# A streaming encoder step on one core: order of the last feed-forward part, PSUM copies for the GELU inputs, and projections woven between recurrent branches

## The chip, the core and the metric

The kernel runs on one core of a Trainium2 chip. A core has five engines that run side by side and meet through semaphores: TensorE (PE, matrix products into PSUM; PEld are its weight loads), VectorE (DVE), ScalarE (ACT), GpSimd (POOL) and SyncE (SP), which here issues all DMA transfers. Each engine executes its own list of instructions strictly in the order written; an instruction that waits holds up everything behind it on that engine. The metric is the device time of one execution in microseconds (us), taken as the median of several.

## The reference

One step of a two-layer encoder with 1024 columns of a prompt and 64 columns of a sample that continues a cache. Layer 0 mixes with two kinds of attention (A and B); layer 1 mixes with forgetting attention (C) and a gated recurrent branch (D). A gated feed-forward network (FFN) follows each mixer, and a norm ends it.

```python
def rmsnorm(x, g):
    return x * lax.rsqrt(jnp.mean(x * x, axis=-1, keepdims=True) + EPS) * g
def swiglu(h, w1, w3, w2):
    return (jax.nn.silu(h @ w1) * (h @ w3)) @ w2
# layer 1, mixer C and D
    cq, ck, cv, cf, dx, dg = split_cols(h @ w_in, CD_SIZES)
    logf = log_sigmoid(cf + c_f_bias); F = jnp.cumsum(logf, axis=1)
    # C: s = q k^T * SCALE + F_q - F_k, causal softmax, times v (8 heads)
    # D: width-4 causal convolution u of dx, then for every channel
    r = sigmoid(u @ w_a + b_a); i = sigmoid(u @ w_x + b_x)      # blocks of 64
    log_a = -RG_C * r * softplus(-lam); a = exp(log_a)
    b = sqrt(-expm1(2.0 * log_a)) * (i * u)                     # h_t = a_t h_(t-1) + b_t
    o_d = hseq * gelu(dg)
    out = concatenate([o_c, o_d]) @ w_out
# each layer: x += mixer(rmsnorm(x)); x += swiglu(rmsnorm(x)); at the end rmsnorm(x)
```

All values are fp32. The model width is 1024, the recurrent width 512, the FFN's hidden width 2816.

## The kernel before, in words

The 1088 columns (1024 of the prompt and 64 of the sample) lie along the free dimension and are cut into three chunks of 384, 384 and 320 columns (`CH`). Features lie on the partitions, in blocks of 128. Every large product is made of three matrix multiplications on rounded halves (high times high, high times low, low times high), so an output block of one chunk with 8 input blocks costs 24 matmuls; this text calls that a chunk product. `split` makes such halves: ACT copies the high half (L217) and another engine subtracts it (L218). `loadw` loads a weight block with one DMA into a ring of two raw buffers, and then splits it: ACT L217, POOL L218.

The order of the program: `layer_ab` (attention A and B and its output product), `ffn(0)`, `layer_cd` (the four recurrent branches, then four C units of two heads each, then the output product), `ffn(1)`, the final norm. The program is written as Python code; a scheduler turns it into one list per engine, and these lists are fixed before the run. Matmul results go to a ring of eight PSUM banks in the FFN (`mmf`) and in the recurrent branches (`mmd`), and to a ring of two banks (`mma`) in the projections of attention units.

*Last FFN part.* `ffn` adds the second product in three parts of hidden blocks. Parts 0 and 1 go block by block, all three chunks with each weight block. The last part, of 6 blocks (L1126 to L1128, 18 matmuls for a block and chunk), goes chunk by chunk: for each chunk all eight output blocks, each with its own load of the weight block (`second`, 128x768), 24 loads in all. DVE adds the result to x (L1156); ACT squares it, and DVE or POOL adds up the squares (`addsq`, L274 and L275). After output block 3 of chunks 1 and 2 stands `rms` of the chunk before: one matmul over the partitions (L256), then Ln and Exp on ACT. After chunk 1 comes `after(0, ..)`: in layer 0 that is `between`, which loads the first weights of layer 1 (`early_weights`), stores x of the chunk and norms it (`norm`: DVE L284, split on ACT, DVE and POOL). The rest (`rms` of chunk 2, and chunks 1 and 2 of `between` or `final`) comes after.

*Recurrent branches.* For m = 0 to 3, `d_in` computes dx of branch m (a chunk product for each chunk, L234 to L236) and ACT copies it from PSUM (L1272); `d_conv` makes u from it on DVE (four passes and a split); `d_gelu` computes the gate product dg (L234 to L236) and GELU of it: Square on ACT (L1282), POOL L1283, DVE L1284, Tanh on ACT (L1287, L1289), DVE L1290. For branches 1 to 3 the operand of Square, L1284 and L1290 is the PSUM bank itself; for branch 0 ACT copies it to SBUF first. `d_close` multiplies u with the two gate matrices (L1317 to L1319, 18 matmuls), takes Sigmoid on ACT (L1320), then goes on: POOL L1328, ACT Tanh (L1330), Exp, Square, Ln, Exp (L1335 to L1339), DVE, the scan over time on DVE (L1342, L1343) and the product with the gate (L1346); its result is stored in `o_spill`. The program's order is d_in(m), d_close(m-1), d_conv(m), d_gelu(m).

*First attention unit.* `units` then runs the projections q, k and v of the first C unit (`proj`, L246, 24 matmuls for a chunk). `d_close` of branch 3 is put in where k's weights are loaded. From then on `run` weaves the items of one attention unit (scores L457 and L458, DVE L469, Exp on ACT, transposes L574, value products L499 and L500) with the projections of the next unit. Before the first scores the bias of the unit's two heads must be there: two loads of `forget_rows` (stored earlier by the forget scan) and POOL L762; that bias lies where the buffers of the last branch lay.

## Time and profile before

Three executions took 2762.43, 2769.10 and 2769.78 us (median 2769.1). The profile is of one more execution that took 2767.11 us; its span on the core, from first to last instruction, is 2765.3 us, so 1.8 us lie around it.

| | us | share of span |
|---|---|---|
| PE matmuls | 2613.0 | 94% |
| DVE | 1367.8 | 49% |
| POOL | 1253.5 | 45% |
| ACT | 1222.7 | 44% |
| chain that ended last, steps on PE | | 76% |
| mean clock granted to PE | | 0.979 |

Busy time counts the time in which an engine has an instruction in hand. The chain is followed back from the last instruction to what released it each time. The span is long and has many stages; the change touches the stretch from about 1350 to 1640 us (end of the first FFN, recurrent branches, first attention unit) and the last 60 us, and the text reads those stretches on their own. In rows of groups, the columns are line, engine, operation, output and input with their shapes, count, then busy us and mean ns of one, then idle time of the engine just before and what ended it. In rows of the timeline they are start, duration and the instruction, with the idle time before it and what ended that in brackets.

### The profile page before, as it was taken

To read this page: it belongs to the slowest core of one execution; us is meant where nothing else is said; L and a number is where in the kernel's file an instruction comes from. 1 tells how busy PE (TensorE), PEld (TensorE's weight loads), DVE (VectorE), ACT (ScalarE), POOL (GpSimd) and SP (SyncE) were. 2 spreads that over 40 slices of the span, in tenths; PEclk is the share of its full clock that TensorE was granted. 3 is DMA by queue.
4 is the path that set the end of the run, shared out by engine and by line. 5 is a ranking of instruction groups with operands and counts; after the bars stand their busy time and mean duration, and the time that the engine had idled before them with its cause. 6 is when DMAs were issued, how large, how long until landed. Compare 5 with 4: busy or idle time off the path is not lost.

```text
span 2765.3 us, 45216 instructions
## 1 busy us (share of the span) xinstructions
PE 2613.0 (94%) x17614; PEld 2536.4 (92%) x17614; DVE 1367.8 (49%) x2739; ACT 1222.7 (44%) x2395; POOL 1253.5 (45%) x990
## 2 busy tenths in 40 slices
PE   6999999988899999999988789998989999999997
PEld 5899999888899999999978779988989999999997
DVE  7666666767332332522257547777853233242225
ACT  5666677754323323311245546676432323331113
POOL 5222222323766676312474333352466667642135
PEclk9999999999999999999999899999999999999998
DMA  6222222352222221532342432234222221244224
GB/s 203 73 68 77 68 64 58 109 156 72 81 95 71 81 84 63 186 110 78 101 148 34 46 89 80 76 121 149 94 78 87 79 87 63 87 149 139 71 66 144
DMA packets 119287, 261.63 MB, mean 95 GB/s; under 512 B 21896, under 2 KB 71312, under 8 KB 119072
## 3 DMA queue, kind: packets, MB, share of 16 engines
q1 hardware_dynamic: 119072, 258.74, 30.8%
q8 instruction: 138, 2.26, 0.3%
q14 instruction: 77, 0.63, 0.1%
HBM read 190.49 MB, written 65.43 MB: 93 GB/s over the span
## 4 chain that ended last, share of the span: by engine, by line
PE 76%; DVE 8%; ACT 6%; DMA 4%; POOL 3%; issue 3%; SPq 0%; DVEq 0%; ACTq 0%; POOLq 0%
PE banks L1026 32%; PE banks L246 16%; PE banks L1127 6%; PE banks L1128 6%; PE banks L1126 6%; PE banks L574 3%; ACT split_arena L217 2%; DVE split_arena L218 2%; POOL split_arena L218 2%; PE banks L457 2%; PE banks L458 1%; PE banks L499 1%; PE banks L500 1%; DMA arena<-o_spill 1%; DVE arena L275 1%
## 5 line engine op out<-in xcount | busy, mean ns | idle before, releaser
L218 POOL TENSOR_TENSOR split_arena<-arena,split_arena 128x512 fp32r<-128x512 f32 (+5 forms) x530 | 824.5, 1559 | 1176.0 <-ACT split_arena L217 1099.4
L217 ACT ACTIVATE split_arena<-arena 128x512 fp32r<-128x512 f32 (+10 forms) x693 | 486.6, 714 | 1111.8 <-PE banks L1026 441.0
L1026 PE MATMUL banks<-split_arena 128*128 128x272 f32 x7392 | 946.3, 291 | 29.0 <-DVE split_arena L218 13.3
L1026 PEld LDWEIGHTS banks<-split_arena 128*128 128x128 f32 x7392 | 941.1, 190 | 34.2 <-DVE split_arena L218 14.8
L246 PE MATMUL banks<-split_arena 128*128 128x384 f32 (+1 forms) x3528 | 663.1, 335 | 23.3 <-DVE arena L1290 8.0
L246 PEld LDWEIGHTS banks<-split_arena 128*128 128x128 f32 x3528 | 587.3, 191 | 32.6 <-DVE arena L1290 8.3
L1126 PE MATMUL banks<-split_arena 128*128 128x384 f32 (+1 forms) x1056 | 347.3, 329 | 5.2 <-DVE arena L1093 3.6
L1128 PE MATMUL banks<-split_arena 128*128 128x384 f32 (+1 forms) x1056 | 347.1, 329 | 3.6 <-POOL split_arena L218 3.6
L1127 PE MATMUL banks<-split_arena 128*128 128x384 f32 (+1 forms) x1056 | 346.3, 328 | 1.7 <-DVE split_arena L218 1.7
L218 DVE TENSOR_TENSOR split_arena<-banks,split_arena 128x512 fp32r<-128x512 f32 (+4 forms) x312 | 167.6, 542 | 96.8 <-ACT split_arena L217 93.9
L1126 PEld LDWEIGHTS banks<-split_arena 128*128 128x128 f32 x1056 | 199.7, 189 | 7.5 <-issue 4.0
L1128 PEld LDWEIGHTS banks<-split_arena 128*128 128x128 f32 x1056 | 199.8, 189 | 5.0 <-POOL split_arena L218 4.9
L1127 PEld LDWEIGHTS banks<-split_arena 128*128 128x128 f32 x1056 | 199.8, 189 | 2.4 <-DVE split_arena L218 2.0
L218 DVE TENSOR_TENSOR split_arena<-arena,split_arena 128x1088 fp32r<-128x1088 f32 (+8 forms) x163 | 163.4, 1013 | 76.8 <-ACT split_arena L217 75.9
L469 DVE CUSTOM_DVE_ANT_0 arena<-banks,arena 128x384 f32<-128x384 f32 (+4 forms) x368 | 175.6, 494 | 45.7 <-PE banks L458 39.8
L217 ACT ACTIVATE split_arena<-banks 128x512 fp32r<-128x512 f32 (+4 forms) x312 | 146.6, 476 | 106.5 <-PE banks L574 45.3
L1034 DVE TENSOR_TENSOR arena<-banks,arena 128x544 f32<-128x544 f32 (+1 forms) x46 | 32.1, 699 | 301.2 <-PE banks L1026 301.2
L1147 DVE TENSOR_TENSOR arena<-banks,arena 128x384 f32<-128x384 f32 (+1 forms) x96 | 51.3, 535 | 251.4 <-PE banks L1128 251.2
L471 ACT ACTIVATE arena<-arena 128x640 f32<-128x640 f32 (+8 forms) x216 | 156.3, 724 | 43.3 <-DVE arena L469 41.9
L574 PE MATMUL banks<-arena 128*128 128x128 f32 (+2 forms) x828 | 134.1, 273 | 14.1 <-DVE arena L490 7.1
L574 PEld LDWEIGHTS banks<-arena 128*128 128x128 f32 (+2 forms) x828 | 95.9, 140 | 31.5 <-DVE arena L490 10.5
L457 PE MATMUL banks<-split_arena 128*128 128x256 f32 (+3 forms) x312 | 112.7, 363 | 3.0 <-issue 2.0
(167 smaller groups left out, 3059.7 us busy)
## 6 DMA issues: line engine op xcount, KB each, us to landing
arena<-in_w_dram SPq DMA_DIRECT2D x120, 512.0 KB, 3.5
h_spill<-arena SPq DMA_DIRECT2D x22, 1088.0 KB, 4.2
arena<-h_spill SPq DMA_DIRECT2D x44, 544.0 KB, 4.7
arena<-in_w_dram SPq DMA_DIRECT2D x48, 384.0 KB, 3.2
arena<-in_abw_dram SPq DMA_DIRECT2D x24, 512.0 KB, 3.7
arena<-in_cdw_dram SPq DMA_DIRECT2D x20, 512.0 KB, 3.9
x_spill<-arena SPq DMA_DIRECT2D x48, 192.0 KB, 2.2
arena<-x_spill SPq DMA_DIRECT2D x16, 544.0 KB, 4.9
```

What stands on the lines that cost most here:

```text
L217: self.nc.scalar.activation(hi, x, AF.Copy)
L218: return sub.tensor_tensor(lo, x, hi.bitcast(F32), op=ALU.subtract)
L246: self.pe = self.nc.tensor.matmul(ps, x[:, k], y[k][:, c0:c0 + n], start=a and i == 0, stop=z and i == 2).ins
L457: nc.tensor.matmul(ps[:, :mw], qd[:, q0:q0 + m], kk[:, k0 + s:k0 + s + mw], start=True, stop=False)
L469: nc.vector.tensor_tensor_reduce(o, p, t, -1.0, low, ALU.add, ALU.min, to)
L471: nc.scalar.activation(sb, sb, AF.Exp, bias=st[:, 0:1], scale=-1.0, accum_out=st[:, 1:2])
L574: nc.tensor.transpose(pt[:r, t * nq + s * m:t * nq + s * m + m], src, self.ident[:m, :m])
L1026: nc.tensor.matmul(bank[:, p], l[:, k], r[:, k, x], start=first and i == 0, stop=k == 3 and i == 2, skip_group_check=True)
L1126: nc.tensor.matmul(ps, wh, h[:, c0:c0 + n], start=j == j0, stop=False)
L1127: nc.tensor.matmul(ps, wh, lo[:, c0:c0 + n], start=False, stop=False)
L1128: nc.tensor.matmul(ps, wl, h[:, c0:c0 + n], start=False, stop=j == j1 - 1)
L1147: nc.vector.tensor_tensor(xs, ps, xs, op=ALU.add)
```

## The change

Three things are done.

1. **Last FFN part.** Its loop goes over the eight output blocks with chunks 0 and 1 each, then over blocks 6 and 7 (whose weights are still there) and 0 to 5 (loaded again) with chunk 2: 14 loads of a weight block where there were 24. `rms` of chunks 0 and 1 both stand after the second block of chunk 2, followed by `after(0, ..)`, and in layer 1 also `after(1, ..)` two blocks later. Adding up squares in chunk 2 is given to DVE for the first three blocks and alternates after that. The first weights of layer 1 are loaded while blocks 3 and on are computed.
2. **GELU inputs.** `d_gate` (new) computes dg of branches 1 to 3 and ACT copies it from PSUM to SBUF (L1319 of the new program). GELU of branch m-1 is computed from that copy in the next turn, after the gate products of m-1. `d_close` is cut into `d_gates` (products and Sigmoid) and the rest. The ring of the branches' weights has three places instead of four.
3. **First attention unit.** Its six chunk products of q and k are computed inside the recurrent branches, two in each turn (q0 and q1, q2 and k0, k1 and k2), through the eight-bank ring. `d_gates(3)`, GELU of branch 3 and the rest of branch 3 stand ahead of the v projection, which is all that is left of `proj` for this unit.

No product is added or removed: the number of matmuls is the same, 17,579.

```diff
-        self.w_d = at([0, 1024, R_V[0], R_PT]), at([2048, 3072, R_V[1], R_PT + 1024])
+        self.w_d = at([0, 1024, R_PT]), at([2048, 3072, R_PT + 1024])
...
-    def proj(self, u, d, wq, wk, wv, pair, outs):
+    def proj(self, u, d, wq, wk, wv, pair, outs, only_v=False):
...
-        w = self.loadw(wq, self.w_a)
...
+        if not only_v:
+            w = self.loadw(wq, self.w_a)
...
-    def clear_ql(self):
...
             self.start(d, *units[0][2])
-            nb = units[0][1]()
         else:
-            for kind, _ in self.proj(0, d, *units[0][2]):
-                if kind == "w" and between:
-                    between(self.pe)
-                    between = None
-            nb = units[0][1]()
+            for kind, _ in self.proj(0, d, *units[0][2], True):
+                if kind == "w":
+                    between()
+                    self.clear_ql(1)
+        nb = units[0][1]()
...
-    def ffn(self, l, after):
+    def ffn(self, l, after, early=lambda: None):
...
-        more = [(ci, m) for ci in range(3) for m in range(8)]
-        lasts = []
...
                 xs = self.x[m][ci]
                 nc.vector.tensor_tensor(xs, ps, xs, op=ALU.add)
-        rs = []
-        for ci, (c0, n) in enumerate(CH):
-            for m in range(8):
-                if 8 * ci + m + 1 < len(more):
-                    lasts.append(second(2, more[8 * ci + m + 1][1], ends, nc.gpsimd))
+
+        blocks = list(range(8)) + list(range(6))
+        uses = [(i, (0, 1)) for i in range(8)] + [(i, (2,)) for i in range(6, 14)]
+        ws.append(second(2, 1, ends, nc.gpsimd))
+        for q, (i, cs) in enumerate(uses):
+            if q + 2 < 9 or q > 8:
+                m = len(ws)
+                if m < 14:
+                    ws.append(second(2, blocks[m], ends, nc.gpsimd))
+            if q == 3:
+                early()
+            m = blocks[i]
+            for ci in cs:
+                c0, n = CH[ci]
                 ps = self.mmf.get()[:, :n]
-                gemm2(ps, lasts.pop(0), 2, c0, n)
+                gemm2(ps, ws[i], 2, c0, n)
                 xs = self.x[m][ci]
                 nc.vector.tensor_tensor(xs, ps, xs, op=ALU.add)
                 if ci < 2:
                     self.addsq(ci, m, xs, (nc.vector, nc.gpsimd)[m % 2])
+                elif q < 11:
+                    self.addsq(2, m, xs, nc.vector, first=q == 8)
                 else:
-                    self.addsq(ci, m, xs, (nc.gpsimd, nc.vector)[m % 2], 2 - 2 * (m % 2), m < 2)
-                if ci > 0 and m == 3:
-                    rs.append(self.rms(ci - 1))
-            if ci == 1:
-                after(0, rs[0])
+                    self.addsq(2, m, xs, (nc.gpsimd, nc.vector)[q % 2], 2 - 2 * (q % 2), q == 11)
+            if q == 9:
+                r0 = self.rms(0)
+                r1 = self.rms(1, to=self.v(F_END, 384))
+                after(0, r0)
+            if q == 11 and l:
+                after(1, r1)
 
         def rest():
-            r = self.rms(2, [2, 0], self.acc[1])
-            after(1, rs[1])
+            r = self.rms(2, [2, 0], self.v(F_END + 384, 384))
+            if not l:
+                after(1, r1)
             after(2, r)
         return rest
 
     def between(self, ci, r):
         c0, n = CH[ci]
-        if ci == 0:
-            self.early_weights()
         for k in range(8):
             self.dma(self.xTd[k * 128:k * 128 + 128, c0:c0 + n], self.x[k][ci])
         self.norm(ci, 8, r=r)
...
-        b["uh"], b["ul"] = self.r(R_Q[m % 2], T), self.r(R_Q[m % 2] + T, T)
+        b["uh"], b["ul"] = (self.r(o, T) for o in ((R_Q[1], R_Q[1] + T), (R_Q[1] + 2 * T, R_QL[1]))[m % 2])
...
-        nc.scalar.activation(dx[:, 3 + c0:3 + c0 + npr], ps[:, :npr], AF.Copy)
+        b["in"] = nc.scalar.activation(dx[:, 3 + c0:3 + c0 + npr], ps[:, :npr], AF.Copy).ins
...
-    def d_gelu(self, b, ci, ps=None):
+    def d_gelu(self, b, ci):
         nc = self.nc
         c0, n = CH[ci]
-        if ps is None:
-            ps, _ = self.d_products(b["w"][1], ci)
+        ps = b["G"][:, c0:c0 + n]
         z2, z = self.stg.get()[:, :n], self.nat.get()[:, :n]
         nc.scalar.activation(z2, ps, AF.Square)
...
-    def d_close(self, b, m, after):
-        nc, O = self.nc, self.O
+    def d_gate(self, b):
+
+        for ci, (c0, n) in enumerate(CH):
+            ps, _ = self.d_products(b["w"][1], ci)
+            self.nc.scalar.activation(b["G"][:, c0:c0 + n], ps, AF.Copy)
+
+
+    def d_gates(self, b, m, after):
+        nc = self.nc
         R = self.D.get()
         b["slots"].insert(0, R)
-        R, u = R[:, 0:T], b["u"]
-        Ig = b["dx"][:, 0:T]
+        b["R"] = R = R[:, 0:T]
+        b["I"] = Ig = b["dx"][:, 0:T]
         for gi, (dst, bc) in enumerate(((R, 5), (Ig, 6))):
             hi, lo = self.gates[2 * m + gi]
             for c0, n in CH:
...
+    def d_close(self, b, m):
+        nc, O = self.nc, self.O
+        R, Ig, u = b["R"], b["I"], b["u"]
...
-    def recurrent(self, pending):
+    def recurrent(self, pending, d, wq, wk, ckT, outs, keep):
...
-        gates = []
         for ci in range(3):
             (p, _), f, (g, _) = step(ci) if ci else first
...
-        for ci in range(3):
-            self.d_gelu(b, ci, gates[ci])
+        stg, self.stg2 = self.stg, Ring(self.M, [F_STG2, F_STG2 + 384], 384)
+
+        def between():
+
+            w = self.loadw(wq, [Ring(self.MR, [R_K[0] + 1024 * i], 1024) for i in range(2)])
+            for ci in range(3):
+                ps, _ = self.d_products(w, ci)
+                self.put_q(d, *CH[ci], ps)
+                if ci == 1:
+                    v = self.loadw(wk, [Ring(self.MR, [R_V[i]], 1024) for i in range(2)])
+                    self.cached_k(d, ckT)
+                yield
+            for ci in range(3):
+                ps, _ = self.d_products(v, ci)
+                self.stg = self.stg2
+                self.new_k(d, *CH[ci], ps, outs, keep)
+                self.stg = stg
+                yield
+        self.clear_ql(0)
+        more = between()
         for m in range(1, 4):
             nb = self.d_open(m)
             for ci in range(3):
                 self.d_in(nb, ci)
-            self.d_close(b, m - 1, nb["pe"])
+            next(more)
+            self.d_gates(b, m - 1, nb["pe"])
+            with self.tc.issue_after(nb["in"]):
+                for ci in range(3):
+                    self.d_gelu(b, ci)
+            self.d_gate(nb)
+            self.d_close(b, m - 1)
+            next(more)
             self.d_conv(nb, m)
+            b = nb
+
+        def rest():
+            self.d_gates(b, 3, b["pe"])
             for ci in range(3):
-                self.d_gelu(nb, ci)
-            b = nb
-        return lambda after: self.d_close(b, 3, after)
+                self.d_gelu(b, ci)
+            self.d_close(b, 3)
+        return rest
 
     def layer_cd(self, pending):
         nc, I, O = self.nc, self.I, self.O
         W = I["cdw"]
         self.lastu = 3
-        rest = self.recurrent(pending)
+        rest = self.recurrent(pending, self.qkv_views(0), W[0], W[4], I["cckT"][0], (O["c_kT"][0], O["sc_kT"][0]), 0)
```

The lists of the engines are the same up to the last FFN part of layer 0. Three places show what moves after it.

On DVE at the turn from chunk 1 to chunk 2 of the last FFN part of layer 0 (sum with x: L1156 before, L1165 now; adding squares: L275, now L277; norm of chunk 0: L284 and L218, now L286 and L220), before:

```order
L284 SCALAR_TENSOR_TENSOR arena<-arena 128x384
L218 TENSOR_TENSOR split_arena<-arena,split_arena 128x384
L1156 TENSOR_TENSOR arena<-banks,arena 128x384
L284 SCALAR_TENSOR_TENSOR arena<-arena 128x384
L275 TENSOR_TENSOR arena<-arena 128x384
L284 SCALAR_TENSOR_TENSOR arena<-arena 128x384 x2
L1156 TENSOR_TENSOR arena<-banks,arena 128x384
L218 TENSOR_TENSOR split_arena<-arena,split_arena 128x384
L284 SCALAR_TENSOR_TENSOR arena<-arena 128x384 x2
L218 TENSOR_TENSOR split_arena<-arena,split_arena 128x384
L1156 TENSOR_TENSOR arena<-banks,arena 128x320
```

and now:

```order
L1165 TENSOR_TENSOR arena<-banks,arena 128x384
L277 TENSOR_TENSOR arena<-arena 128x384
L1165 TENSOR_TENSOR arena<-banks,arena 128x384 x2
L1165 TENSOR_TENSOR arena<-banks,arena 128x320 x2
L277 TENSOR_TENSOR arena<-arena 128x320
L286 SCALAR_TENSOR_TENSOR arena<-arena 128x384 x3
L220 TENSOR_TENSOR split_arena<-arena,split_arena 128x384
L1165 TENSOR_TENSOR arena<-banks,arena 128x320
L220 TENSOR_TENSOR split_arena<-arena,split_arena 128x384
```

The norm's first products and splits stood ahead of the first sum of chunk 2 (128x320); two of these sums and one of its squares now stand ahead of them.

On ACT in the turn of a recurrent branch (Sigmoid of the gates: L1320, now L1337; copies of dx from PSUM: L1272, now L1284; Square and Tanh of GELU: L1282, L1287, L1289, now L1293, L1298, L1300; the chain behind the gates: L1330 to L1339, now L1351 to L1360), before, from the end of one chain to the next gates:

```order
L1282 ACTIVATE arena<-banks 128x384
L217 ACTIVATE split_arena<-arena 128x1024
L1287 ACTIVATE arena<-arena 128x384
L1282 ACTIVATE arena<-banks 128x320
L1289 ACTIVATE arena<-arena 128x384
L1289 ACTIVATE arena<-arena 128x320
L1272 ACTIVATE arena<-banks 128x384 x2
L217 ACTIVATE split_arena<-arena 128x1024
L1272 ACTIVATE arena<-banks 128x256
L1274 ACTIVATE arena<-banks 128x64
L1320 ACTIVATE arena<-banks,arena 128x384 x2
```

and now, from the middle of a chain on:

```order
L1360 ACTIVATE arena<-arena 128x384
L1319 ACTIVATE arena<-banks 128x384
L1360 ACTIVATE arena<-arena 128x384
L1357 ACTIVATE arena<-arena 128x320
L219 ACTIVATE split_arena<-arena 128x1024
L1359 ACTIVATE arena<-arena 128x320
L219 ACTIVATE split_arena<-arena 128x64
L1360 ACTIVATE arena<-arena 128x320
L1293 ACTIVATE arena<-arena 128x384
L1319 ACTIVATE arena<-banks 128x320
L219 ACTIVATE split_arena<-arena 128x1024
L176 ACT_TABLE_LOAD
```

GELU's Square read the bank itself between the products; now a copy of the bank (L1319) stands there, among the steps of the chain, and Square reads SBUF.

On PE from the last gate products to the first scores of the first attention unit (gates: L1317 to L1319, now L1334 to L1336; projections: L246, now L248; transposes of v: L356 and L359, now L358 and L361; scores: L457 and L458, now L460 and L461), before:

```order
L1318 MATMUL banks<-split_arena 128x320
L1319 MATMUL banks<-split_arena 128x320
L246 MATMUL banks<-split_arena 128x384 x48
L246 MATMUL banks<-split_arena 128x320 x48
L246 MATMUL banks<-split_arena 128x384 x4
L356 MATMUL banks<-arena 128x128 x2
L246 MATMUL banks<-split_arena 128x384 x8
L359 MATMUL banks<-arena 64x128
L246 MATMUL banks<-split_arena 128x384 x17
L356 MATMUL banks<-arena 128x128 x3
L246 MATMUL banks<-split_arena 128x384 x19
L457 MATMUL banks<-split_arena 64x320
```

and now:

```order
L1335 MATMUL banks<-split_arena 128x320
L1336 MATMUL banks<-split_arena 128x320
L248 MATMUL banks<-split_arena 128x320 x24
L248 MATMUL banks<-split_arena 128x384 x24
L460 MATMUL banks<-split_arena 64x320
L358 MATMUL banks<-arena 128x128 x2
L248 MATMUL banks<-split_arena 128x384 x15
L358 MATMUL banks<-arena 128x128 x2
L361 MATMUL banks<-arena 64x128
L358 MATMUL banks<-arena 128x128
L248 MATMUL banks<-split_arena 128x384 x9
L461 MATMUL banks<-split_arena 64x320
```

Behind the last gate products stood the products of k and v; now v's stand there alone (24 of 320 columns and 48 of 384), and the next rows belong to the second unit's q.

42 lines of the change are left out of this document (22 added, 20 removed).

## The prediction

> **What bounds the kernel now.** I read the chain of waits first, then cut the span into stages by time, then asked who PE waited for in the stage that changes. Page, chain that ended last:
>
> ```profile
> PE 76%; DVE 8%; ACT 6%; DMA 4%; POOL 3%; issue 3%; SPq 0%; DVEq 0%; ACTq 0%; POOLq 0%
> ```
>
> PE sets the end, so a gain must be idle or slow time of PE. Stage by stage (stretch, its length, busy us of PE, PEld, DVE, ACT, POOL with counts, granted clock, DMA share, GB/s):
>
> ```profile
> 1403.80:1436.70 32.90, 22.90 (x128) 20.92 (x129) 17.98 (x23) 14.66 (x27) 24.18 (x20) 0.84 0.52 148
> 1483.00:1519.70 36.70, 28.81 (x168) 27.65 (x168) 26.36 (x30) 22.10 (x43) 13.11 (x13) 0.98 0.22 31
> 1519.70:1554.70 35.00, 29.76 (x163) 28.71 (x163) 21.29 (x22) 19.07 (x37) 14.98 (x10) 0.92 0.37 47
> 1554.70:1579.20 24.50, 15.63 (x84) 15.11 (x84) 15.92 (x22) 17.16 (x35) 5.71 (x7) 0.87 0.36 44
> 1597.50:1639.20 41.70, 32.44 (x175) 30.79 (x173) 16.59 (x23) 19.56 (x41) 17.84 (x19) 0.92 0.35 98
> 1403.80:1639.20 235.40, 190.16 (x1055) 180.15 (x1055) 139.32 (x170) 120.30 (x243) 106.42 (x104) 0.92 0.36 72
> 2727.00:2751.50 24.50, 19.54 (x126) 18.20 (x124) 11.88 (x19) 10.10 (x17) 14.37 (x9) 0.98 0.44 140
> 2751.50:2765.30 13.80, 2.50 (x4) 1.18 (x4) 5.54 (x8) 2.49 (x5) 3.85 (x4) 0.50 0.35 124
> ```
>
> From the last FFN chunk of layer 0 to the first attention scores PE is idle 235.4 - 190.2 = 45 us, and slowed while busy (clock 0.84 and 0.87). No other engine is full there. Its waits in that stretch (waiter, releaser, total, times, longest):
>
> ```profile
> PE banks L1317 <- DVE arena L1290: 8.7, 4, 3.7
> PE banks L246 <- DVE arena L1290: 8.0, 1, 8.0
> PE banks L256 <- POOL arena L275: 6.6, 1, 6.6
> PE banks L246 <- ACT split_arena L304: 6.3, 2, 4.0
> PE banks L356 <- DVE arena L350: 2.9, 1, 2.9
> ```
>
> PE waits for PSUM banks that GELU holds (L1290) and for the squares of a chunk (L256 on L275). Both are what the change works on.
>
> **Last FFN part of layer 0.** Timeline rows of PE, and groups between 1403.8 and 1436.7:
>
> ```profile
> 1399.77 0.33 PE L1128 MATMUL banks<-split_arena 128*128 128x384 f32 x1
> 1400.81 0.33 PE L1128 MATMUL banks<-split_arena 128*128 128x384 f32 x1
> 1400.99 0.31 PE L1126 MATMUL banks<-split_arena 128*128 128x320 f32 x1
> 1403.47 0.31 PE L1128 MATMUL banks<-split_arena 128*128 128x320 f32 x1
> 1410.43 1.65 PE L256 MATMUL banks<-arena 128*128 128x384 f32 x2 [6.65 <-POOL arena L275]
> 1416.29 0.47 PE L1127 MATMUL banks<-split_arena 128*128 128x320 f32 x1
> 1418.95 0.47 PE L1128 MATMUL banks<-split_arena 128*128 128x320 f32 x1
> ```
>
> ```profile
> L218 POOL TENSOR_TENSOR split_arena<-arena,split_arena 128x768 fp32r<-128x768 f32 x7 | 12.9, 1843 | 6.4 <-ACT split_arena L217 6.4
> L217 ACT ACTIVATE split_arena<-arena 128x768 fp32r<-128x768 f32 x7 | 5.9, 841 | 9.3 <-DMA arena<-in_w_dram 9.3
> L284 DVE SCALAR_TENSOR_TENSOR arena<-arena 128x384 f32<-128x384 f32 x8 | 8.7, 1123 | 0.2
> ```
>
> A matmul of 384 columns starts every 1.04/6 = 0.173 us, one of 320 every 2.48/17 = 0.146; after the 6.65 us stall 2.66/10 = 0.266. Hence a chunk product of 24 costs 4.16 or 3.51 us, three chunks 11.8, the 18 gate products 3.0. Chunk 2 has 8 x 18 matmuls, 21.0 us, and with the two `rms` 22.7. It ran from 1400.99 to 1436.7, 35.7 us. So 13.0 us is all that can be got. Now weights come 14 times, not 24: with chunks 0 and 1 a block lasts 18 x 2 x 0.173 = 6.2 us on PE against 1.84 on POOL and 0.84 on ACT for its split, and the first two blocks of chunk 2 need no load. But chunk 0's norm, eight L284 of 1.12 us with splits between them, now begins 6 blocks (15.8 us) ahead of the branches' first product: about 9 us of L284 and 4 splits and sums leave 0 to 4 us uncovered, and POOL's last squares may hold `rms` a little. I take a gain of **10** (5 to 13).
>
> **The recurrent turns.** PE rows, with idle time in brackets:
>
> ```profile
> 1483.24 0.44 PE L1317 MATMUL banks<-split_arena 128*128 128x384 f32 x1 [0.97 <-ACT split_arena L217]
> ...
> 1579.24 1.01 PE L246 MATMUL banks<-split_arena 128*128 128x384 f32 x2 [8.01 <-DVE arena L1290]
> ...
> 1597.48 0.34 PE L1317 MATMUL banks<-split_arena 128*128 128x384 f32 x1
> ```
>
> From the end of d_in(1), 0.97 us ahead of the first row, to gates(3) it takes 1597.5 - 1482.3 = 115.2 us. After the change PE has there three gates (3 x 3.0), d_in of branches 2 and 3, dg of 1 to 3, and q and k: 9 + 7 x 11.8 = 91.6 us. One turn (35.0 us above, with 26.6 us of products: two times 11.8 and 3.0) gains two chunk products, about 8 us, which is what its GELU chain left open. A bank of dg is freed by one copy and not after a whole GELU; the chain behind it no longer stands in front of PE. Left are waits for weights (L217, L218) and for u; the small ones now, about 1 us each (0.97 above), come three to five times: 2.7 (0 to 8). So gates(3) come 115.2 - 91.6 - 2.7 = **20.9** us earlier over and above the first part (15 to 24).
>
> Three copies a branch are added on ACT, which is busy 19.1 of 35.0 us in such a turn; a copy is of Square's kind (0.5 us), 1.5 us a turn. It hides behind ACT's idle 15.9 us; uncovered it would cost 4.5.
>
> **From gates(3) to the scores.** What is late next is the closing chain of branch 3, for the bias of the first scores lies in its buffers. Rows of ACT, DVE, SP (start, issue time) and POOL in order of time, and GELU's Tanh as a group:
>
> ```profile
> 1599.54 0.76 ACT arena L1320 x2
> ...
> 1613.95 2.99 DVE L1342 TENSOR_TENSOR_SCAN arena<-arena 128x1024 f32<-128x1024 f32 x1
> 1617.93 3.42 DVE L1346 SCALAR_TENSOR_TENSOR arena<-arena 128x1088 f32<-128x1088 f32 x1
> 1621.38 0.33 SPq L170 DMA_DIRECT2D o_spill<-arena  x1
> 1632.04 0.33 SPq L170 DMA_DIRECT2D arena<-forget_rows  x1
> 1636.61 0.31 POOL L762 TENSOR_TENSOR arena<-arena 64x64 f32<-64x64 f32 x1 [5.64 <-DMA arena<-forget_rows]
> 1639.23 0.47 DVE L469 CUSTOM_DVE_ANT_0 arena<-banks,arena 64x320 f32<-64x320 f32 x1
> ```
>
> ```profile
> L1289 ACT ACTIVATE arena<-arena 128x384 f32<-128x384 f32 x4 | 2.1, 524 | 7.3 <-DVE arena L1284 7.3
> ```
>
> 41.7 us pass from gates(3) to the first score. None of it is removed, and GELU of branch 3 is now inside it (six ACT passes of about 0.5 us: 3 us, with DVE's and POOL's parts beside them), and the chain of branch 2, whose gates stand only 18 us of products ahead (3.0, dg 11.8 and the last of k 3.5), runs into it. Behind the waiting score on DVE stand all later scores, and Exp on ACT waits for them. I take **4** us longer (1 to 8). PE has less under it: it was busy 32.4 of those 41.7 us; now it has the gates, v (11.8) and 30 matmuls of the second unit's q (5.2), 20 in all, and waits 25 us. Those 30 stood behind the first scores before; they fill idle time and are saved later, as far as PE bounds the unit: **3** us gained (0 to 5). PE then starts slow, as after the 6.65 us stall, where some 20 matmuls cost 0.12 us more: **2** lost (1 to 3).
>
> **End of layer 1.** The last 8 blocks of chunk 2 take 24.5 us now, limited by their loads; at 2.63 us each they take 21.0. But DVE gets 16 products of the final norm in front of the sums of chunk 2, and after the last product `rms`, `final` and its stores (13.8 us above) stay as they are. I take **1** gained (4 gained to 2 lost).
>
> **Sum.** -10 - 20.9 + 4 - 3 + 2 - 1 = -29, so 2738 against the profiled execution's own 2767.1. Its median is 2769.1, 2.0 above it; I state the forecast for the median: **2740**.
>
> **A rule against it.** Two sums of squares on DVE, of 384 and 320 columns:
>
> ```profile
> 1403.44 0.56 DVE L275 TENSOR_TENSOR arena<-arena 128x384 f32<-128x384 f32 x1
> ...
> 1426.22 2.06 DVE L275 TENSOR_TENSOR arena<-arena 128x320 f32<-128x320 f32 x1 [0.54 <-ACT arena L274]
> ```
>
> The second, smaller one ran beside POOL's L218 and took 1.5 us longer. The Trainium skill, SBUF — State Buffer, "SBUF: two separate sides", says that a DVE instruction with two SBUF inputs and a GpSimd instruction exclude each other for their whole length; a PSUM operand avoids that. These rows agree. As a mechanism here: L1284 and L1290 had one operand in PSUM, now both lie in SBUF. If each of branch 3's six is held by 1.5 us, its chain grows by 9 us, to 2749.
>
> **The rivals.** *(a) The held GELU*: the closing chain of branch 3 grows by six times 1.5 us on top of the 4: 2740 + 9 = 2749. For it: the pair of rows. Against it: POOL is busy only 15.0 of 35.0 us in a turn. *(b) PE full*: no stall in the turns, all 13 us of the FFN, and the scores wait no longer than before: -13 - 23.6 - 5 + 2 - 4 = -43.6 from 2769.1, 2726. Against it: each weight load still comes in order behind others on SP. *(c) ACT's list as the bound, slower than before.* The copies that free dg's banks stand among the steps of the closing chain on ACT. That chain takes from Sigmoid to scan some 14 us (1599.5 to 1613.9) and waits for POOL and DVE inside. If a copy must wait for it in each of three turns and the eight banks are full by then, a turn is its 35 us of products and 14 of chain: 3 x 14 = 42 lost on top of the other terms, 2740 + 42 = 2782. It decides once the chain ends more than the turn's later products (dg's two chunks, 8 us, and q or k's, 4) after the copy's bank is full. Against it: these banks and products give 12 us of slack of those 14. *(d) The change does not do what it says*: the scheduler's lists show q and k within the turns, so only the FFN's part might fail, if `rms` waits as before: 2740 + 10 = 2750.
>
> **How the numbers follow.** Chances: forecast 0.62 (own range 2728 to 2752), (a) 0.14, (b) 0.08, (c) 0.08, (d) 0.08. The range of 8 in 10 takes in (a), (d) and part of (b), and the bad ends of the turns and the FFN (6 + 5 us) with the better part of the closing chain's: 2724 to 2759. What can be told from no change here is 0.3%, 8.3 us: faster means under 2760.8. Of (c) I put 0.07 slower and 0.01 within; of the forecast, (a) and (d) 0.08 fall within, where their bad ends meet. Faster 0.84, same 0.09, slower 0.07.
>
> **What would show it.** Right: chunk 2 of the first FFN's last part within 27 us; waits of PE for L1290's successor gone; turns of 35 to 38 us with PE over 95%; gates(3) near 1567; the first score near 1612, with PE idle over 20 us ahead of it. Wrong: PE waiting for a dg copy that follows a chain step on ACT (c); L1290's successor at 2 us (a); the first score within 42 us of gates(3) (b); `rms` still waiting over 5 us (d). The forecast fails most easily at the 20.9 of the turns, should PE wait for u or a weight load.

## The result and the profile after

The changed kernel takes 2751.15 us (median of 4, 2749.40 to 2753.34) against 2769.44 us (4 runs) before. The ratio is 0.9933, 95% interval 0.9921 to 0.9945: faster by 18 us (15 to 22). The forecast was 2740 (2724 to 2759): the direction and the range hold, and 11 us of the gain are missing.

The profiled execution of the change took 2753.34 us, the slowest of its four and 2.2 above their median; that of the kernel before lay 2.3 below its own. So the two spans, 2765.3 and 2751.6, differ by 13.7 only, and 13.7 + 2.2 + 2.3 = 18.2 is the difference of the medians. The steps below add up to the 13.7 but for rounding. The page of the change, engines and chain that ended last:

```profile
span 2751.6 us, 45123 instructions
PE 2614.3 (95%) x17614; PEld 2541.5 (92%) x17614; DVE 1353.8 (49%) x2741; ACT 1209.4 (44%) x2384; POOL 1223.8 (44%) x968
PE 9%; DVE 0%; ACT 0%; DMA 0%; POOL 0%; DVEq 0%; issue 0%; ACTq 0%; SPq 0%
```

PE is as busy as before (2613.0), with 17,614 matmuls in both profiles (17,579 above is not what they count), so idle time went. The chain is of no use here: its shares add up to 9%, so it was not followed back to the stretch that changed. The stages have to be cut by time again. The change by stage (columns as in the prediction; the third row takes in the tail of the second):

```profile
1401.00:1428.30 27.30, 25.51 (x167) 24.72 (x165) 18.92 (x22) 13.97 (x25) 17.50 (x14) 1.00 0.44 128
1428.30:1481.40 53.10, 49.81 (x294) 45.91 (x293) 36.19 (x54) 26.61 (x57) 27.95 (x33) 1.00 0.25 52
1477.20:1585.20 108.00, 95.67 (x560) 94.14 (x558) 66.36 (x70) 66.44 (x133) 46.55 (x36) 0.95 0.36 51
1528.70:1565.30 36.60, 35.39 (x212) 35.07 (x211) 19.79 (x24) 21.42 (x44) 14.47 (x13) 1.00 0.47 63
1585.20:1626.60 41.40, 27.29 (x135) 25.59 (x135) 22.65 (x33) 22.79 (x52) 19.79 (x20) 0.84 0.46 90
```

The marks between the stages are first products of PE: d_in(0), gates(3), and the first score on DVE. The end of d_in(1) is that of its last product.

| stretch | before | after | difference | forecast |
|---|---|---|---|---|
| up to d_in(0) | 1436.7 | 1428.3 | -8.4 | -10 |
| d_in(0) to the end of d_in(1) | 45.6 | 48.9 | +3.3 | 0 |
| end of d_in(1) to gates(3) | 115.2 | 108.0 | -7.2 | -20.9 |
| gates(3) to the first score | 41.8 | 41.4 | -0.4 | +4 |
| first score to the end | 1126.1 | 1125.0 | -1.1 | -2 (-3 + 2 - 1) |

The first line came nearly as forecast: from the first product of chunk 2 (1403.84) it takes 24.5 us where it took 35.7, and `rms` no longer waits. These 11.2 us show as 8.4 in the table because chunk 2 begins 2.8 us later in this profile than before (1401.0). That is not shown to come from the change: in the profiles of the twelve kernels here that have the new order, chunk 2 begins between 1398.4 and 1403.8, so single profiles of one order differ there by 5 us. Of the second line 3 us are PE waits for the halves of chunk 1's norm (the two L237 lines below). The hole is in the third. PE has 91.6 us of products there and took 108.0: 12.3 idle, and 4.1 in which products ran slower than their usual pitch. The turn from 1528.7 to 1565.3 shows what was forecast: 36.6 us with PE busy for 35.4, 97%. Who PE waited for from 1401 to 1640:

```profile
PE banks L236 <- DVE split_arena L329: 9.6, 2, 8.4
PE banks L460 <- DVE arena L472: 8.0, 1, 8.0
PE banks L248 <- ACT arena L1337: 3.1, 1, 3.1
PE banks L237 <- DVE split_arena L220: 2.4, 1, 2.4
...
PE banks L237 <- POOL split_arena L220: 0.6, 1, 0.6
```

One wait of 8.4 us stands out. It is in the first of the new turns, at the second chunk of dg(1), and slows PE after it. PE's rows:

```profile
1499.04 0.69 PE L236 MATMUL banks<-split_arena 128*128 128x384 f32 x1 [8.42 <-DVE split_arena L329]
1499.53 0.52 PE L237 MATMUL banks<-split_arena 128*128 128x384 f32 x1
...
1504.01 0.45 PE L236 MATMUL banks<-split_arena 128*128 128x384 f32 x1
1504.30 0.34 PE L237 MATMUL banks<-split_arena 128*128 128x384 f32 x1
1504.47 0.33 PE L238 MATMUL banks<-split_arena 128*128 128x384 f32 x1
```

From 1499.53 to 1504.01 stand 14 products 0.32 us apart, then 0.17 again: 14 times 0.15 is 2.1 us lost on top of the 8.4.

The bank that PE needs holds the first product of q, which came first in this turn; L329 of `put_q` is the instruction that has read it last. What stood ahead of L329 on DVE:

```profile
1484.55 5.16 DVE L1244 TENSOR_TENSOR_SCAN arena<-arena 8x1024 f32<-8x1024 f32 x2 [0.24 <-DMA out_c_logfT_dram<-arena]
1489.74 0.99 DVE L1245 TENSOR_SCALAR arena<-arena 8x1344 f32<-8x1344 f32 x1
...
1492.79 0.55 DVE L1295 TENSOR_TENSOR arena<-arena 128x384 f32<-128x384 f32 x1
1496.00 0.56 DVE L1295 TENSOR_TENSOR arena<-arena 128x384 f32<-128x384 f32 x1 [2.66 <-POOL arena L1294]
1496.48 1.35 DVE L1311 SCALAR_TENSOR_TENSOR arena<-arena 128x1091 f32<-128x1091 f32 x1
1497.86 1.12 DVE L329 SCALAR_TENSOR_TENSOR split_arena<-banks,split_arena 64x384 fp32r<-64x384 f32 x2
```

First the forget scan (L1244, 5.2 us, and L1245), then passes of branch 1's convolution (L1311). Behind it GELU's L1295, which then waits for POOL's L1294. POOL and SP in the same microseconds:

```profile
1489.12 0.91 POOL L1294 TENSOR_SCALAR arena<-arena 128x384 f32<-128x384 f32 x1
1495.28 0.10 POOL L1269 MEMSET arena<- 128x3 f32 x1 [5.25 <-DMA forget_rows<-arena]
1495.46 0.51 POOL L1294 TENSOR_SCALAR arena<-arena 128x384 f32<-128x384 f32 x1
...
1531.53 0.10 POOL L1269 MEMSET arena<- 128x3 f32 x1 [12.79 <-DMA o_spill<-arena]
```

```profile
1490.76 0.27 SPq L172 DMA_DIRECT2D forget_rows<-arena  x1
```

L1269 sets three zero columns ahead of branch 2's dx. It lasts 0.1 us, but its buffer is the one that the forget values lay in, and it must wait until these are stored: the store is issued when the scan is done and lands 4.5 us later. POOL's list stands still for 5.25 us, so GELU's L1294 does, so DVE's L1295, so L329, so PE. In the next turn the same instruction, for branch 3 in branch 0's buffer, waits 12.8 us for the store of branch 0's result. And put_q's copies on ACT stand behind L1298, which waits for the first L1295:

```profile
1493.38 0.52 ACT L1298 ACTIVATE arena<-arena 128x384 f32<-128x384 f32 x1 [5.33 <-DVE arena L1295]
1493.81 0.47 ACT L324 ACTIVATE split_arena<-banks 64x384 fp32r<-64x384 f32 x1
1494.30 0.49 ACT L325 ACTIVATE split_arena<-banks 64x384 fp32r<-64x384 f32 x1
```

### The profile page after: what moved, and what is told of

Read it like the earlier page. It is cut to its first block, busy times and chain, and to the rows that moved or that the text cites. A ratio compares the mean times of both kernels' runs of the same rounds, so it can differ in the third digit from the quotient of the medians.

```text
span 2751.6 us, 45123 instructions
## 1 busy us (share of the span) xinstructions
PE 2614.3 (95%) x17614; PEld 2541.5 (92%) x17614; DVE 1353.8 (49%) x2741; ACT 1209.4 (44%) x2384; POOL 1223.8 (44%) x968
## 5 line engine op out<-in xcount | busy, mean ns | idle before, releaser
L220 POOL TENSOR_TENSOR split_arena<-arena,split_arena 128x512 fp32r<-128x512 f32 (+5 forms) x510 | 798.1, 1569 | 1196.9 <-ACT split_arena L219 1121.6
L219 ACT ACTIVATE split_arena<-arena 128x512 fp32r<-128x512 f32 (+8 forms) x673 | 469.9, 710 | 1054.2 <-PE banks L1028 439.5
L248 PE MATMUL banks<-split_arena 128*128 128x384 f32 (+1 forms) x3384 | 641.3, 336 | 5.6 <-ACT arena L1337 3.1
L248 PEld LDWEIGHTS banks<-split_arena 128*128 128x128 f32 x3384 | 565.4, 192 | 13.7 <-ACT arena L1337 3.4
L1128 PE MATMUL banks<-split_arena 128*128 128x384 f32 (+1 forms) x1056 | 347.0, 329 | 6.3 <-DVE arena L1095 4.3
L1130 PE MATMUL banks<-split_arena 128*128 128x384 f32 (+1 forms) x1056 | 346.8, 329 | 5.9 <-POOL split_arena L220 5.9
L1129 PE MATMUL banks<-split_arena 128*128 128x384 f32 (+1 forms) x1056 | 346.5, 328 | 0.0
L220 DVE TENSOR_TENSOR split_arena<-banks,split_arena 128x512 fp32r<-128x512 f32 (+4 forms) x312 | 167.4, 541 | 95.7 <-ACT split_arena L219 92.9
L220 DVE TENSOR_TENSOR split_arena<-arena,split_arena 128x1088 fp32r<-128x1088 f32 (+8 forms) x163 | 161.4, 1001 | 76.8 <-ACT split_arena L219 76.0
L1147 DVE TENSOR_TENSOR arena<-banks,arena 128x384 f32<-128x384 f32 (+1 forms) x96 | 51.3, 534 | 258.5 <-PE banks L1130 258.3
L236 PE MATMUL banks<-split_arena 128*128 128x384 f32 (+1 forms) x312 | 107.2, 345 | 16.2 <-DVE split_arena L329 9.6
```

Of the source, the lines that this page charges most:

```text
L219: self.nc.scalar.activation(hi, x, AF.Copy)
L220: return sub.tensor_tensor(lo, x, hi.bitcast(F32), op=ALU.subtract)
L236: nc.tensor.matmul(ps, wh[:, k], hh[k][:, c0:c0 + n], start=(k == ks[0]), stop=False)
L248: self.pe = self.nc.tensor.matmul(ps, x[:, k], y[k][:, c0:c0 + n], start=a and i == 0, stop=z and i == 2).ins
L1128: nc.tensor.matmul(ps, wh, h[:, c0:c0 + n], start=j == j0, stop=False)
L1129: nc.tensor.matmul(ps, wh, lo[:, c0:c0 + n], start=False, stop=False)
```

## The experiments

The theory (F in e4, Q in e5, e6 and e9 in the texts on record): the turns missed their time because on DVE, POOL and ACT work that is not urgent (the forget scan; zero columns in a reused buffer that waits for a store) stands in front of what frees q's bank. Rivals: one, that whatever is taken away, the next serial wait of the same turn takes its place, so the time stays (L in e9, S in e11); another, that it is the place of q's product and its bank in the ring of eight that costs (B); a third, that the loss is not in the turns but in the bias that the first scores wait for (E). In e1 and e2 the letters S and P name something else: two ways in which the gain could split between the parts. Each kernel has the time of the kernel before from the same chip beside it; comparisons across kernels go by the ratios. All kernels compute everything.

**One part alone.** The first kernel is the one before with part 1 (the FFN's order), the second the changed one with the old order of the FFN.

```diff
...  (e1, against the kernel before; e2, against the change, has the reverse)
-        more = [(ci, m) for ci in range(3) for m in range(8)]
...
+        blocks = list(range(8)) + list(range(6))
+        uses = [(i, (0, 1)) for i in range(8)] + [(i, (2,)) for i in range(6, 14)]
```

> The kernel before with the new last FFN part alone. Theory S (the shift seen in the changed kernel's trace passes to the end): the last chunk product of d_in(1) ends 5 us earlier there, and behind it the branches are a chain of waits that keeps its length, so 2769.4 - 5 - 1 for the last FFN = 2763. Rival P (the forecast's term was right and the weave ate it): the part gains 10 us by itself, 2759 or less. Rival N: the branches' waits absorb the shift, 2768 to 2769.

> The changed kernel with the old last FFN part (copies and woven q and k kept). Theory S: the branches' part is worth 18 - 6 = 12 us, 2757. Theory P: 8 us, 2761. If the two parts only work together (the weave needs the early start): no gain, 2769.

e1: 2758.31 against 2766.66, ratio 0.9973 (0.9963 to 0.9983), 8 us (5 to 10). e2: 2758.79, ratio 0.9972 (0.9962 to 0.9983), also 8. The two add up to 16, about the 18 of both: the parts do not hinder each other. The FFN's part is worth what was forecast less a little; the copies and the weave together are worth 8 where the forecast's terms for them sum to 18.

**The copies without the weave.** q and k go back into `proj`; the order of the FFN, the GELU copies and `d_gates` stay.

```diff
-            for kind, _ in self.proj(0, d, *units[0][2], True):
+            for kind, _ in self.proj(0, d, *units[0][2]):
...
-            next(more)
             self.d_gates(b, m - 1, nb["pe"])
```

> The changed kernel with q and k back in the projection step ahead of the first scores; copies of the GELU inputs and the new FFN part stay. If the banks held by GELU were the cause of the 28 us of waits, the copies alone shorten a turn from 35 to nearly the 27 us of its products and the first scores come as early as in the changed kernel: 2751. If the chain of a branch (conv, gates, Sigmoid, scan) sets the turn, the turns stay 30 to 35 us and q and k come on top: 2757 to 2763.

2760.46, ratio 0.9980 (0.9970 to 0.9989): no better than the FFN's part alone. PE's waits in this kernel, 1425 to 1640:

```profile
PE banks L1335 <- ACT split_arena L219: 23.7, 3, 13.6
PE banks L248 <- ACT split_arena L306: 5.9, 2, 4.0
PE banks L248 <- DVE split_arena L329: 5.3, 1, 5.3
```

A bank that comes free early brings nothing here: the gates (L1335) then wait 23.7 us in three pieces for u's halves, the end of the chain of a branch through conv. What pays is the work that stands in this gap, the q and k products: with them the ratio goes from 0.9980 to 0.9933, about 13 us.

**The forget scan later.** Its call is moved behind `d_close` of branch 0, and its buffer to a place of its own.

```diff
-        Lf = self.v(F_S, 1344)[0:8]
+        Lf = self.v(F_END, 1344)[0:8]
...
-        self.forget(Lf)
...
             self.d_close(b, m - 1)
+            if m == 1:
+                self.forget(Lf)
```

> The changed kernel with the forget values in a buffer of their own and their scan put behind the first turn's chain. Theory F: the stall of 8.4 us of PE in turn 1 comes from DVE, where the forget scan and the wait for its store stand ahead of the instruction that frees the bank of q's first chunk; then the stall is gone, with some 3 us of slow clock behind it, and gates(3) and the first score come about 11 us earlier: 2740. Rival B: eight banks are too few for q in front of six gate products, whoever is late; then PE waits for Sigmoid instead and the time stays at 2749 to 2751. Rival C: the scan only moves to the next turn and delays u there: 2745 to 2751.

2749.10, ratio 0.9944 (0.9930 to 0.9959): no gain. The kernel did not become what it was meant to be: the scheduler, which orders each list by its own costs, left the scan where it was on DVE; only the buffer moved. PE:

```profile
1492.73 0.69 PE L236 MATMUL banks<-split_arena 128*128 128x384 f32 x1 [5.67 <-DVE split_arena L329]
...
1533.16 0.69 PE L236 MATMUL banks<-split_arena 128*128 128x384 f32 x1 [3.01 <-DVE split_arena L329]
```

8.42 became 5.67, and 1.21 in the next turn became 3.01. With the values in a place of their own, POOL no longer waits for their store in the first turn, so that store is one part of the stall; what is left of it has the scan still ahead of L329. In the second turn POOL's memset waits 13.2 us for the store of branch 0's result, as it did in the change (12.8).

**Zero columns and scan out of the way.** The next two kernels write the zero columns on ACT in front of the copies of dx, and give the forget values their own place; the second also forces the scan behind branch 0's closing chain.

```diff
-        self.nc.gpsimd.memset(b["dx"][:, 0:3], 0.0)
...
+        if ci == 0:
+            nc.scalar.activation(dx[:, 0:3], self.zero[:, 0:3], AF.Copy)
...  (e6 only)
+            last = self.d_close(b, m - 1)
+            if m == 1:
+                with self.tc.issue_after(last):
+                    self.forget(Lf)
```

> The changed kernel with the forget values in a buffer of their own, and the three zero columns in front of dx written by ACT ahead of the first copy of dx, not by POOL when the branch is opened. Theory Q (lists in order): POOL's zeroing of the next branch waits there for a store (of the forget values in turn 1, of a branch's result in turn 2) and GELU's step on POOL, DVE's steps and the release of q's banks stand behind it; then the stalls of PE of 8.4 and 1.2 us become about 5.5 (the scan alone is left) and 0, and the first score comes 4 to 6 us earlier: 2745. Rival D: DVE alone is too full in turn 1 and POOL does not matter: no change, 2749 to 2751.

> The kernel of the run before with the forget scan held on DVE behind the closing chain of branch 0 (6.2 us of scan and negation). Theory Q with DVE's list as the second part of the stall in turn 1: nothing of the 8.4 us is left beyond 1 us; the scan falls into turn 2 where DVE idles 5 us ahead of the next conv: 2741. Rival D2: the scan costs the same 6 us one turn later, as u of branch 2 then comes late: 2745.

e5: 2749.73 against 2767.52, ratio 0.9941 (0.9925 to 0.9956). e6: 2748.62, ratio 0.9935 (0.9919 to 0.9950). Neither can be told from the change. In e6 the stall of the first turn fell to 3.06, but a new one came:

```profile
1488.40 0.69 PE L236 MATMUL banks<-split_arena 128*128 128x384 f32 x1 [3.06 <-DVE split_arena L329]
...
1523.39 0.64 PE L1335 MATMUL banks<-split_arena 128*128 128x320 f32 x1 [3.37 <-ACT arena L1285]
```

Its cause is the edit itself. ACT of e6:

```profile
1522.75 0.20 ACT L1284 ACTIVATE arena<-arena 128x3 f32<-128x3 f32 x1 [15.54 <-DMA o_spill<-arena]
1522.87 0.47 ACT L1285 ACTIVATE arena<-banks 128x384 f32<-128x384 f32 x1
```

The three columns of branch 3 still wait for the store of branch 0's result, now on ACT: the scheduler put them far forward, and ACT stood still for 15.5 us behind a copy of 0.2. So e5 and e6 do not test the theory cleanly: they move that wait from POOL to ACT and do not take it away. At this point the moving stall (L) looked right.

**The bias of the first head earlier.** It gets a place of its own, and the buffer of branch 3's gate a slot that is free sooner.

```diff
-        t = self.v(F_BIAS + 1344 * (h % 2), 1344)
+        t = self.v(F_BIAS + 1344 * (h % 2) if h else F_END, 1344)
...
+        if m == 3:
+            i = next(i for i, s in enumerate(self.D.free) if s is self.D.all[2])
+            self.D.free.insert(0, self.D.free.pop(i))
```

> The changed kernel with the bias of the first unit's two heads out of the reach of branch 3's buffers (head 0 in free space, and branch 3's R in slot 2, so that head 1's place is free early). Theory E: the 8 us for which PE waits ahead of the first scores are the wait for the bias, which is loaded behind the closing chain and its stores; with it loaded early the first scores run beside the closing chain, and the time falls by 8 to 13 us: 2737 to 2742. Rival H: the first scores are held by DVE's and ACT's lists (v's splits and the chain itself stand there too), and the chain of branch 3 takes as long later, where its result is not urgent: 3 us gained, 2747. Rival C: the scores between push the closing chain back and PE waits later for it: no gain.

2748.01 against 2767.52, ratio 0.9930 (0.9912 to 0.9947): the same as the change. The first score comes 30.0 us after gates(3) where it came 41.4, yet from there to the end it takes 1135.0 in place of 1125.0. PE of e7 says why:

```profile
1591.79 4.33 PE L248 MATMUL banks<-split_arena 128*128 128x384 f32 x15 [5.59 <-ACT split_arena L306]
1603.97 7.44 PE L248 MATMUL banks<-split_arena 128*128 128x320 f32 x33 [7.86 <-ACT arena L1340]
```

Ahead of the scores PE waits for copies of k (L306, in `put_k`) and for Sigmoid of branch 3 (L1340). The second of these waits is the edit's own: ACT's record of L1340 at 1603.34 had waited 8.73 us for the store of branch 2's result into `o_spill`, because slot 2, which the edit gives to branch 3's gate, is where that result lies. e8, e9 and e10, which have the same edit, show this wait too (7.42, 8.45 and 4.73 us); the kernels without it do not. So e7 met the same trap once more, and it does not decide what an earlier bias alone would be worth.

**All together, and with the zero columns in their place.** e8 is e6 and e7 in one. e9 differs from e8 only in that the three columns stand behind the previous branch's copies on ACT's list.

```diff
...
         if ci == 0:
-            nc.scalar.activation(dx[:, 0:3], self.zero[:, 0:3], AF.Copy)
+            with self.tc.issue_after(self.copied):
+                nc.scalar.activation(dx[:, 0:3], self.zero[:, 0:3], AF.Copy)
...  (self.copied is the last copy of the branch before)
```

> All of the three runs before in one kernel. If the terms add: 2750 less 9 (turns) less 10 (bias) = 2731. If they meet the same limit (the first unit's ACT and DVE work): 2738.

> The kernel with all three edits, with one flaw of it mended: in e6 and e8 the zero columns of branch 3 had come on ACT ahead of branch 2's copies from PSUM and waited there 15 us for the store of branch 0, which lies in the same slot; now they stand behind the copies of the branch before. Theory Q (whatever waits for a store on an in-order engine stalls PE through the banks): the 3.4 to 4.9 us that PE then waited in turn 2 go, and the slow clock after them: 2745 - 5 = 2740. Rival L (the turn is bound by the sum of steps between u of one branch and u of the next, so that a stall taken away comes back at the next wait): 2744 to 2746.

e8: 2745.07 against 2767.52, ratio 0.9921 (0.9905 to 0.9936). e9: 2738.46 (2734.04 to 2741.70) against 2767.69, ratio 0.9896 (0.9879 to 0.9912): 29 us faster than before, and its interval lies wholly below that of the change. This version beats both kernels. e8's copy on ACT, and then PE's waits in e9 from 1425 to 1640:

```profile
1525.24 0.20 ACT L1284 ACTIVATE arena<-arena 128x3 f32<-128x3 f32 x1 [15.47 <-DMA o_spill<-arena]
```

```profile
PE banks L248 <- ACT arena L1342: 7.3, 1, 7.3
PE banks L248 <- ACT split_arena L306: 5.6, 1, 5.6
PE banks L237 <- DVE split_arena L220: 2.4, 1, 2.4
...
PE banks L1339 <- DVE split_arena L329: 1.3, 1, 1.3
...
PE banks L236 <- DVE split_arena L329: 0.5, 1, 0.5
```

Of the waits on L329 in the turns 0.5 and 1.3 us are left, where they were 8.4 and 1.2. The stretch that was forecast at 94.3 us, end of d_in(1) to gates(3), in e9:

```profile
1475.70:1571.70 96.00, 92.69 (x560) 91.85 (x558) 67.14 (x71) 62.83 (x127) 42.30 (x32) 1.00 0.39 57
```

96.0 us against 108.0 in the change, with the same 560 products, idle for 3.3 and at full clock. This is what the theory says: with the scan, the memset and the copy out of the way the turns nearly take their products' time. About 3 us of it is not the edits' doing: in e9 PE came later to the first turn, as the stretch ahead of it, d_in(0) to the end of d_in(1), took 51.3 us where e8 has 47.4.

The two full turns, gates(0) to gates(1) and gates(1) to gates(2), show where the time went, in us:

| kernel | first turn | second turn |
|---|---|---|
| the change | 47.3 | 36.6 |
| e4 | 44.0 | 39.8 |
| e5 | 43.7 | 40.9 |
| e6 | 39.8 | 41.9 |
| e8 | 38.2 | 43.3 |
| e9 | 35.2 | 36.7 |

What e4, e5, e6 and e8 took from the first turn came back for the most part in the second, as (L) says, where the wait for the store of branch 0's result stands (on POOL in e4, on ACT by the edit itself in e5, e6 and e8). With the copy in its place it no longer did, so (L) held for the single steps and not for all of them together. The third rival (E), that the loss is not in the turns, falls here as well: e8 and e9 have the same bias, and they differ in the turns. That one copy (e8 to e9) is worth 6.6 us in the second turn, and 6.6 us between medians from two chips; between the ratios it is 2.5 thousandths, and their intervals overlap a little.

**Is it q's place?** Here q's product stands behind dg, so that its bank cannot be in dg's way: once on top of e9, once on the change alone.

```diff
-            next(more)
             self.d_gates(b, m - 1, nb["pe"])
...
             self.d_gate(nb)
+            next(more)
```

> The same with the first woven product of each turn behind the next branch's gate-input products instead of ahead of the gates. The gates of a branch then come 4 us earlier and no bank of q or k stands in front of the next branch's copies. Theory B (banks held by q's slow release are what is left in turn 1, 3.1 us): 2 to 4 us faster than e9. Rival U (the six gate products then meet the copies without cover, and PE waits for Sigmoid): same or up to 5 us slower than e9.

> The changed kernel with only that order: the first woven product of a turn behind the gate-input products. Theory B: the 8.4 us stall falls to what Sigmoid's wait for the store of the forget values leaves, 4 to 6 us, 2747. Rival S (Sigmoid, not q, then holds the banks, since it waits for the same scan and store): the stall stays at about 8 us at another place, 2750 to 2752.

e10: 2739.32, ratio 0.9899 (0.9882 to 0.9917), as e9. e11: 2750.08, ratio 0.9938 (0.9922 to 0.9953), as the change. So B falls: no gain or loss from the place of q can be told. PE of e11:

```profile
1489.33 0.63 PE L236 MATMUL banks<-split_arena 128*128 128x320 f32 x1 [3.74 <-ACT arena L1337]
...
1602.31 0.66 PE L358 MATMUL banks<-arena 128*128 128x128 f32 x2 [7.33 <-ACT arena L1359]
```

The wait on L329 is gone and others stand in its place (3.7 on Sigmoid, 7.3 on the closing chain), for POOL still waits 6.1 us for the store of the forget values, and DVE 6.5 us for POOL. From the end of d_in(1) to gates(3) e11 takes 103.0 us, 5 fewer than the change, but 44.7 from there to the first score, where the change takes 41.4.

**Chunk 1's norm earlier.** In layer 0 too it is put into the last FFN part, against the 3 us of the second line of the table.

```diff
-            if q == 11 and l:
+            if q == 11:
                 after(1, r1)
...
-            if not l:
-                after(1, r1)
```

> The changed kernel with the norm of chunk 1 in layer 0 issued two blocks after that of chunk 0, as the last norm of layer 1 does it, and not behind the whole FFN. Theory N: the waits of PE in the first branch products (2.4 and 0.6 us for the halves of chunk 1) and the longer stretch ahead of gates(0) go: 2 to 3 us faster than the changed kernel, 2748. Rival V: DVE's sums of chunk 2 come late behind the longer norm and the branches start later: no gain or 2 us slower.

2749.96, ratio 0.9937 (0.9918 to 0.9955): no gain.

```profile
1439.75 1.74 PE L258 MATMUL banks<-arena 128*128 128x320 f32 x4 [2.35 <-POOL arena L277]
```

The waits for the halves were exchanged for one of `rms` on POOL's last squares, which now stand behind the norm.

## Why the prediction was right and where it was wrong

**Last FFN part, -10 (5 to 13): right.** -11.2 from chunk 2's first product on, -8.4 as the table counts it, and 8 (5 to 10) for the whole kernel in e1. What it left out is behind it: it counted 0 to 4 us uncovered for chunk 0's norm, and 3 appeared for chunk 1's, one stretch later.

**The recurrent turns, -20.9 (15 to 24): this is the step that failed.** It measured -7.2. The products were right: 91.6 us were counted, and e9, with PE busy for 92.7, does the stretch in 96.0. The failed clause is "Left are waits for weights (L217, L218) and for u; ... 2.7 (0 to 8)". Measured were 12.3 us of idle time and 4.1 of slow products, 16.4 in place of 2.7, and these 13.7 are the difference to the forecast. The forecast asked whom PE waited for before, and priced those waits; it did not follow the releaser's own list. The new turn makes PE depend on L329 on DVE, in whose list, and in POOL's and ACT's, the order around the change leaves the forget scan and the zero columns ahead. Of the signs set down, gates(3) near 1567 did not come (1585.2), and of the two full turns one took 36.6 us, within the 35 to 38, and the first 47.3. All of that stood in the order of the instructions: that a 0.1 us memset has a store in front of it could be read there, from which buffer it writes.

**GELU's copies: right, and worth nothing alone.** No wait of PE on a dg copy (L1319) is among those of the profile after, so rival (c), ACT's list as the bound of the turns, did not come. But the clause "The chain behind it no longer stands in front of PE" is not what saved time: e3 has the copies and gains nothing by them.

**From gates(3) to the scores, +4 (1 to 8): the mechanism was right, the base wrong.** POOL's row for the first head's bias, before, and then after:

```profile
1630.66 0.31 POOL L762 TENSOR_TENSOR arena<-arena 64x64 f32<-64x64 f32 x1 [6.05 <-DMA arena<-forget_rows]
```

```profile
1626.27 0.31 POOL L765 TENSOR_TENSOR arena<-arena 64x64 f32<-64x64 f32 x1 [8.22 <-DMA arena<-forget_rows]
1626.61 0.48 DVE L472 CUSTOM_DVE_ANT_0 arena<-banks,arena 64x320 f32<-64x320 f32 x1 [9.30 <-POOL arena L765]
```

The bias is there 33.5 us after gates(3) before (1631.0 - 1597.5) and 41.3 after (1626.6 - 1585.2): the closing chain did grow, by 7.9. The slow load of the bias is no part of that growth: it takes 12.6 us here and took 12.3 before. But before, the score came 8.3 us later than its bias, behind products of v on PE; that slack took up the growth. The forecast read the POOL row at 1636.61, which is the second head's, as the one that the first score waited for. So the first score did come within 42 us of gates(3), the sign set down for rival (b), for a reason that is not (b)'s; PE is idle there for 14.1 us, not 25. Its 27.3 busy us are not the 20 forecast: there the clock is 0.84, which alone makes 20 about 24 (20 / 0.84), and 135 products stand there, where the forecast counted 120 (18, 72 and 30).

**30 products of q ahead (-3), slow clock (+2), end of layer 1 (-1).** Together -2 forecast, -1.1 measured from the first score on. They were not measured one by one.

**The rivals.** (a), the held GELU: seen, but small. The GELU steps on DVE, all four branches after, then the three branches before whose operand was in PSUM:

```profile
L1301 DVE SCALAR_TENSOR_TENSOR arena<-arena 128x384 f32<-128x384 f32 (+1 forms) x12 | 10.0, 851 | 3.2 <-ACT arena L1300 3.2
L1295 DVE TENSOR_TENSOR arena<-arena 128x384 f32<-128x384 f32 (+1 forms) x12 | 8.1, 686 | 9.1 <-POOL arena L1294 9.1
```

```profile
L1290 DVE SCALAR_TENSOR_TENSOR arena<-arena,banks 128x384 f32<-128x384 f32 (+1 forms) x9 | 4.5, 526 | 0.6 <-ACT arena L1289 0.6
L1284 DVE TENSOR_TENSOR arena<-banks,arena 128x384 f32<-128x384 f32 (+1 forms) x9 | 4.4, 520 | 0.0
```

They became longer by 0.33 and 0.17 us on average, not by 1.5. The rule cited in the prediction (the Trainium skill, SBUF — State Buffer, "SBUF: two separate sides") agrees in direction: the longest of the twelve took 1.38 us (L1301) and 1.30 (L1295), none over 0.56 before, but the medians are 0.74 and 0.56. How often POOL stood beside them was not counted. (b) did not come, (d) neither: `rms` of the first two chunks no longer waits.

The forecast's sum in spans was -29 and came out as -13.7: 13.7 of the missing 15.3 are the turns'. At the median 11 are missing, since the profiled executions lay 2.3 under and 2.2 over theirs. That e9 gains 29 us, as forecast for the change, is partly chance. In its profile the stretches differ from before by -11.2 in chunk 2, +5.7 up to the end of d_in(1), -19.2 in the turns, -3.1 from gates(3) on, and -1.0 ahead of all that; the second and the fourth were not forecast so.

**What stays open.** From gates(3) on all kernels here but e3, whose q and k stand behind gates(3), take 1161 to 1168 us to the end, whether the first score comes after 27 or 45; which of the waits there (5.6 on L306 and 7.3 on Sigmoid in e9) sets it was not tried, nor an early bias with a slot for branch 3's gate that no store holds. e5, e6 and e8 carry the misplaced zero columns, so that what the scan and the memset cost each by itself is not separated. Nor is the bias's share of e9's gain settled: e8 and e6, which differ by the bias, are 3.6 us apart, with intervals that overlap, and e7 alone gained nothing that can be told. In the profiles e9 takes 1.7 us less than the change from gates(3) on and 12.0 less in the turns.

## What to carry to other kernels

When a change makes an engine wait for a new releaser, read the releaser's list, not only the waits of the engine itself: what stands ahead of the freeing instruction, and for what each of these waits, down to the smallest memset into a buffer whose last content is still being stored. Here such waits came in series, and taking one away showed nothing in the total until the next was gone too, so a change that tests equal can still be half of one that wins. But look whether the next wait was made by the edit itself, as it was in e5 to e8. Freeing a bank early paid here only with other work to put into the gap.

## What the runs showed of the hardware

- An instruction of 0.1 to 0.2 us on 128x3 elements held its engine for 12.8 us (POOL) and 15.5 us (ACT) because its buffer was being stored; nothing behind it on that list moved.
- The first load of `forget_rows`, issued among branch 3's and v's stores, landed after 12.6 us (12.3 before); over the eight loads of that kernel the median is 4.2. In e9, where it is issued among branch 2's and k's stores, none of the eight took over 4.5. What makes the difference was not tried.
- After 8.4 us of idle PE 14 products ran 0.32 us apart, not 0.17, which cost another 2.1 us. The Trainium skill, TensorE: Matmul & The Clock Gate, "Part 1: The HAM clock gate", says that the clock is set by how busy the array has been of late; the rows at 1499.5 (0.32 us apart) and 1504.3 (0.17) agree.
